# A seven-product down projection whose weight sums are made during the up projection and kept in DRAM

## The chip, the cores and the metric

The kernel runs on one core of a Trainium2 chip. The metric is device time of one execution in microseconds (us): the median of the runs shown. The core has five engines with a queue of instructions each: TensorE (PE, matrix products), VectorE (DVE), ScalarE (ACT), GpSimd (POOL) and SyncE (SP, which here only issues transfers between DRAM and the on-chip memory SBUF). An engine works its queue in order; a semaphore holds an instruction until what it needs is there. Products are accumulated in eight banks of PSUM.

## The reference

One encoder block on 512 tokens of width 1024. The part that the change touches is the gated MLP at the end, `D_FF` = 2816:

```python
def conv_ffn(h, w_up, dw_w, dw_b, w_down):
    gu = depthwise_conv(h @ w_up, dw_w, dw_b)
    gate, up = gu[..., :D_FF], gu[..., D_FF:]
    return (jax.nn.silu(gate) * up) @ w_down
...
        x = x + merged @ w_out[l]
        h2 = rms_norm(x, norm2_g[l])
        x = x + conv_ffn(h2, w_ffn_up[l], ffn_dw_w[l], ffn_dw_b[l], w_ffn_down[l])
    return rms_norm(x, norm_f_g)
```

Ahead of it lie a convolution branch and an attention branch, their merge and the product with `w_out`; neither version differs there.

## The kernel before

**Products in three.** Each float32 operand is split into a high and a low half, and a product is made as three matmuls (`mm3`, lines L219, L222, L223: high by high, high by low, low by high). A weight tile of 128x1024 is split by `halve`: ACT copies the high half (L187), DVE subtracts it from the weight to get the low half (L190). Activations are split alike by `split` (ACT L227, DVE L228).

**Weights.** A list `chunks` names all weight tiles in the order of their use. SP loads each into a ring of four buffers called `raw` (L179); `halve` fills a ring of four called `unit`. `weight(name)` prepares the tile asked for and up to two chunks after it. A raw buffer can be loaded again when its last reader is done.

**Up projection.** 44 tiles `wu0` to `wu43` of 24 matmuls 128x512 each. After a tile, ACT (L892) and DVE (L893, L895) do the convolution over tokens; after every second one DVE multiplies gate and up (L900); after every fourth, that is for each of the 11 pairs of inner tiles, POOL makes four sums of activations of 128x256 (`act_sums`, L851 to L854).

**Down projection.** For each pair the two-by-two blocks (tokens by output columns) are multiplied by a scheme with seven products in place of eight. The accumulators are `psd[p, t]`, `p` one of the products 6, 7, 1, 5 and `t` one of two token tiles. A first half (chunks `d1_i`, 24 matmuls a pair) adds to all four; a second half (`d2_i`, 18 matmuls a pair, the last three pairs in another order) goes on in 1, 7 and 5. Between the halves `u2` and `v` are formed from the accumulators (L934 to L936), and POOL adds them to the residual `x1` (L938, three a token tile); the second half's first matmul into a bank waits until its old value was read.

The scheme needs sums of weights. `prep_1` makes two 128x512 sums on DVE (L858, L860) and one on POOL (L859) after the weights' landing, stores one to DRAM (`t2d`, L861) for the second half, then halves (`w_d1b`, `w_d1a`). `prep_2` loads `t2d` and makes a further sum (L870), then halves (`w_d`, `uc`). The order of instructions on each engine is set by the framework's scheduler from the program order and its own estimates.

Of the kernel before, what the change touches and what calls it, by code (L numbers as in the profile page):

```python
# [87 lines left out]
def block_kernel(ctx, tc, xT, xtok, posb, pk, g2b, gfb, w_small, w_a, w_gate, w_q, w_kv,  # L88
# [47 lines left out]
        chunks.append((f"wm{n}", w_mo[n], D))  # L136
    for n in range(KD):
        chunks.append((f"wo{n}", w_o[n], D))
    for n in range(2 * NF):
        chunks.append((f"wu{n}", w_up[n], D))  # L140


    t2d = dram.tile([NPAIR, P, 512], F32, name="t2d")
    for n in range(NPAIR):
        chunks.append((f"d1_{n}", None, 2))
    for n in range(NPAIR):
# [5 lines left out]
    for nm, src, w in chunks:  # L152
        first_raw.append(len(raws))
        first_unit.append(nu)
        if src is not None:
            raws.append((src, w))
            nu += 1
            continue
        n = int(nm[3:])
        if nm[1] == "1":  # L160
            raws.append((w_dn[2 * n], D))
            raws.append((w_dn[2 * n + 1][:, 512:D], 512))
            nu += 2
        else:
            raws.append((w_dn[2 * n + 1], D))
            raws.append((t2d[n], 512))
            nu += 1
# [5 lines left out]
    PREP_AHEAD = 2  # L173

    def load_to(i):
        while len(loaded) <= min(i, len(raws) - 1):
            src, w = raws[len(loaded)]
            raw = wst.tile([P, 1024], F32, tag="raw", name=f"raw{len(loaded)}")
            nc.sync.dma_start(raw[:, :w], src)  # L179
# [15 lines left out]
    def prep_to(i, pin=False):  # L195
        while state["prep"] <= min(i, len(chunks) - 1):
            c = state["prep"]
            r = first_raw[c]
            load_to(r + NRAW - 1)
            nm, src, w = chunks[c]  # L200
            if src is not None:
                u = hold[nm](nm) if nm in hold else unit(nm)
                ready[nm] = halve(u, loaded[r], w, pin)
            else:
                ready[nm] = (prep_1 if nm[1] == "1" else prep_2)(int(nm[3:]), *loaded[r:r + 2])
            state["prep"] += 1
# [641 lines left out]
    def act_sums(i):  # L848

        a, b = act1[i], act2[i]  # L850
        G.tensor_tensor(out=a[:, 2], in0=a[:, 1], in1=b[:, 1], op=ADD)  # L851
        G.tensor_tensor(out=a[:, 3], in0=a[:, 2], in1=a[:, 0], op=SUB)
        G.tensor_tensor(out=a[:, 1], in0=a[:, 0], in1=a[:, 1], op=SUB)
        G.tensor_tensor(out=b[:, 2], in0=b[:, 0], in1=a[:, 3], op=SUB)  # L854

    def prep_1(i, ra, rb_):

        V.tensor_tensor(out=rb_[:, 512:], in0=rb_[:, 0:512], in1=ra[:, 512:], op=SUB)  # L858
        G.tensor_tensor(out=ra[:, 512:], in0=ra[:, 512:], in1=ra[:, 0:512], op=SUB)  # L859
        V.tensor_tensor(out=rb_[:, 0:512], in0=rb_[:, 512:], in1=ra[:, 0:512], op=ADD)  # L860
        nc.sync.dma_start(t2d[i], rb_[:, 0:512])  # L861
        ub = halve(unit(f"d1b_{i}"), rb_, 1024)
        at = asp.tile([P, 2, 4, HS], F32R, tag="as", name=f"as1_{i}")
        split((at[:, 0], at[:, 1]), act1[i])
        ua = halve(unit(f"d1a_{i}"), ra, 1024)
        return at, ua, ub

    def prep_2(i, ra, rb_):

        V.tensor_tensor(out=rb_[:, 0:512], in0=ra[:, 0:512], in1=rb_[:, 0:512], op=SUB)  # L870
        at = dp.tile([P, 2, 3, HS], F32R, tag="as", name=f"as2_{i}")
# [76 lines left out]
    for i in range(NPAIR - LATE):  # L948
        w = weight(f"d2_{i}")
        for p in (1, 7, 5):  # L950
            for t in range(2):
                second(w, t, (p,), stop=i == NPAIR - LATE - 1 and (p, t) == (7, 1))
# [137 lines left out]
```

## Time and profile before

| | us |
|---|---|
| median of 3 runs | 715.92 (715.63 to 716.55) |
| the profiled execution | 718.99 |
| its span, first to last instruction | 717.2 |
| PE busy in the span | 691.9 (96%) |
| DVE, ACT, POOL busy | 513.1, 358.5, 166.2 |
| mean granted TensorE clock | 0.989 of full speed |
| read from and written to DRAM | 74.10 MB, 4.98 MB |

PE is the engine that is nearly always busy. What another engine does shows in the time only where PE waits for it, or where the granted clock of PE falls.

### The profile page before, as it was taken

What the parts mean: (1) busy time and instruction counts of PE and PEld (TensorE: products, weight loads), DVE (VectorE), ACT (ScalarE), POOL (GpSimd) and SP (SyncE); (2) the same over time, 40 slices, a digit from 0 to 9 for tenths busy, and PEclk for the clock granted to TensorE, in tenths of its full rate; (3) what the DMA queues carried; (4) which work ended last, traced back from release to release, by engine and by line L of the source; (5) the groups of instructions that cost most, each with busy time, mean ns of one, the idle gap of its engine ahead of it and who ended that gap; (6) DMA issues with size and microseconds to landing.
All of it is one profiled execution on the core that took longest, in us unless ns stands there. A gap on an engine that the chain in (4) does not pass through costs nothing. (4 is left out here: it accounts for less than half of the span.)

```text
span 717.2 us, 8863 instructions
## 1 busy us (share of the span) xinstructions
PE 691.9 (96%) x3273; PEld 579.0 (81%) x3273; DVE 513.1 (72%) x679; ACT 358.5 (50%) x551; POOL 166.2 (23%) x208
## 2 busy tenths in 40 slices
PE   8999899999999999999999999999999998998994
PEld 8987788888888888888888888888888886786883
DVE  4767799996789986854555654555555679799985
ACT  5758656534688962433344433433333344455552
POOL 1152347702045400001101111101111125123202
PEclk9999999999999999999999999999999999899998
DMA  8803212354310162270133323323322322555533
GB/s 275 313 31 121 85 67 89 106 148 129 89 30 31 59 205 89 89 235 0 59 90 107 97 90 99 107 88 91 116 88 89 104 93 84 175 176 190 181 128 118
DMA packets 26444, 81.76 MB, mean 114 GB/s; under 512 B 3232, under 2 KB 3360, under 8 KB 26400
## 3 DMA queue, kind: packets, MB, share of 16 engines
q1 hardware_dynamic: 25536, 78.30, 33.8%
q10 hardware_dynamic: 864, 2.88, 1.2%
q8 instruction: 26, 0.43, 0.3%
q14 instruction: 18, 0.15, 0.1%
HBM read 74.10 MB, written 4.98 MB: 110 GB/s over the span
## 5 line engine op out<-in xcount | busy, mean ns | idle before, releaser
L223 PE MATMUL pu<-h,w_wu 128*128 128x512 f32 (+2 forms) x360 | 138.7, 385 | 0.0
L222 PE MATMUL pu<-h,w_wu 128*128 128x512 f32 (+2 forms) x360 | 138.7, 385 | 0.0
L219 PE MATMUL pu<-h,w_wu 128*128 128x512 f32 (+2 forms) x360 | 138.3, 386 | 0.3 <-ACT h L227 0.3
L893 DVE SCALAR_TENSOR_TENSOR u<-pu,pkt,u 128x511 f32<-128x511 f32 x44 | 33.0, 749 | 88.0 <-ACT u L892 88.0
L892 ACT ACTIVATE u<-pu,pkt 128x512 f32<-128x512 f32 x44 | 34.2, 777 | 109.9 <-PE pu L223 109.8
L219 PEld LDWEIGHTS pu<-h,w_wu 128*128 128x128 f32 x360 | 67.4, 188 | 13.9 <-ACT h L227 0.5
L223 PEld LDWEIGHTS pu<-h,w_wu 128*128 128x128 f32 x360 | 67.6, 188 | 13.5
L222 PEld LDWEIGHTS pu<-h,w_wu 128*128 128x128 f32 x360 | 67.6, 188 | 13.4
L190 DVE TENSOR_TENSOR w_wu<-raw,w_wu 128x1024 fp32r<-128x1024 f32 x44 | 54.2, 1233 | 4.7 <-ACT w_wu L187 4.7
L491 DVE SCALAR_TENSOR_TENSOR acc<-cv,pkt,acc 128x502 f32<-128x502 f32 (+10 forms) x84 | 57.1, 736 | 0.3
L489 POOL TENSOR_TENSOR cv<-prod,cv 128x510 f32<-128x510 f32 (+4 forms) x32 | 46.3, 1451 | 42.8 <-ACT prod L486 41.2
L851 POOL TENSOR_TENSOR act<-act,act 128x256 f32<-128x256 f32 x11 | 8.8, 796 | 189.7 <-DVE act L900 189.7
L219 PE MATMUL pgt<-hn,w_wg 128*128 128x512 f32 x128 | 50.2, 392 | 0.0
L223 PE MATMUL pgt<-hn,w_wg 128*128 128x512 f32 x128 | 49.9, 389 | 0.0
L222 PE MATMUL pgt<-hn,w_wg 128*128 128x512 f32 x128 | 49.8, 389 | 0.0
L187 ACT ACTIVATE w_wu<-raw 128x1024 fp32r<-128x1024 f32 x44 | 46.2, 1050 | 5.5 <-PE pso L223 2.9
L228 DVE TENSOR_TENSOR as<-act,as 128x1024 fp32r<-128x1024 f32 (+1 forms) x22 | 29.4, 1339 | 11.2 <-ACT as L227 11.2
L227 ACT ACTIVATE as<-act 128x1024 fp32r<-128x1024 f32 (+1 forms) x22 | 20.8, 948 | 30.7 <-PE psd L223 21.2
L895 DVE SCALAR_TENSOR_TENSOR u<-pu,pkt,u 128x511 f32<-128x511 f32 x44 | 33.0, 750 | 1.4
L486 ACT ACTIVATE prod<-cv,pkt 128x510 f32<-128x510 f32 (+4 forms) x32 | 22.9, 717 | 21.3 <-POOL cv L489 19.3
L677 POOL TENSOR_SCALAR pr<-pr,nm 128x512 f32<-128x512 f32 x32 | 22.1, 694 | 42.6 <-DVE nm L676 39.1
L799 POOL TENSOR_TENSOR r<-ssq 128x1 f32<-128x1 f32 x7 | 1.8, 254 | 129.3 <-ACT hp L796 129.3
(288 smaller groups left out, 1690.2 us busy)
## 6 DMA issues: line engine op xcount, KB each, us to landing
raw<-in_w_up_dram SPq DMA_DIRECT2D x44, 512.0 KB, 3.5
raw<-in_w_dn_dram SPq DMA_DIRECT2D x22, 512.0 KB, 3.5
raw<-in_w_gate_dram SPq DMA_DIRECT2D x16, 512.0 KB, 3.4
raw<-in_w_a_dram SPq DMA_DIRECT2D x8, 512.0 KB, 5.1
raw<-in_w_o_dram SPq DMA_DIRECT2D x8, 512.0 KB, 3.5
raw<-in_w_dn_dram SPq DMA_DIRECT2D x11, 256.0 KB, 3.1
t2d<-raw SPq DMA_DIRECT2D x11, 256.0 KB, 3.0
raw<-t2d SPq DMA_DIRECT2D x11, 256.0 KB, 3.5
```

What stands on the lines that cost most here:

```text
L187: x = A.activation(u[:, 0, :w], raw[:, :w], AF.Copy)
L190: x = V.tensor_tensor(out=u[:, 1, :w], in0=raw[:, :w], in1=u[:, 0, :w].bitcast(F32), op=SUB)
L219: i = T.matmul(ps, st[0], mv[0], start=start, stop=False, skip_group_check=go_on)
L222: T.matmul(ps, st[0], mv[1], start=False, stop=False, skip_group_check=go_on)
L223: T.matmul(ps, st[1], mv[0], start=False, stop=stop, skip_group_check=go_on)
L228: V.tensor_tensor(out=pair[1], in0=src, in1=pair[0].bitcast(F32), op=SUB)
L486: x = A.activation(p[:, lo:hi], u[:, lo + d:hi + d], AF.Copy, scale=w)
L489: return G.tensor_tensor(out=acc[:, lo:hi], in0=p[:, lo:hi], in1=acc[:, lo:hi], op=ADD)
L491: return V.scalar_tensor_tensor(out=acc[:, lo:hi], in0=u[:, lo + d:hi + d], scalar=w, in1=acc[:, lo:hi], op0=MULT, op1=ADD)
L892: A.activation(u, ps, AF.Identity, scale=w(1), bias=par("fb", n))
L893: V.scalar_tensor_tensor(out=u[:, 1:S], in0=ps[:, 0:S - 1], scalar=w(0), in1=u[:, 1:S], op0=MULT, op1=ADD)
L895: V.scalar_tensor_tensor(out=u[:, 0:S - 1], in0=ps[:, 1:S], scalar=w(2), in1=u[:, 0:S - 1], op0=MULT, op1=ADD)
```

## The change

A new chunk `d0_k` stands after `wu(4k+2)` in the list. It loads both down tiles of pair k (512 KB each), and DVE makes four sums of 128x512 in place (L217 to L220 of the changed kernel). SP stores both buffers to a DRAM tile `tsum` (L205). `d1_i` and `d2_i` then load finished sums, so `prep_1` and `prep_2` make none. The four activation sums of a pair (now L869 to L872) and the six adds to `x1` (now L950) go from POOL to DVE. The first half takes its products in the order 6, 5, 1, 7. The second half's first two pairs are interleaved. A limit that kept down tiles from being prepared before the last up tile falls away. The matmuls are the same in number and shape.

```diff
+    tsum = dram.tile([NPAIR, 2, P, 1024], F32, name="tsum")
     for n in range(2 * NF):
         chunks.append((f"wu{n}", w_up[n], D))
-    t2d = dram.tile([NPAIR, P, 512], F32, name="t2d")
+        if n % 4 == 2:
+            chunks.append((f"d0_{n // 4}", None, 0))
...
+        wa, wb, ta, tb = w_dn[2 * n], w_dn[2 * n + 1], tsum[n, 0], tsum[n, 1]
+        if nm[1] == "0":
+            raws += [[(wa, 0, D)], [(wb, 0, D)]]
+        elif nm[1] == "1":
+            raws += [[(ta, 0, D)], [(wa[:, 0:512], 0, 512), (tb[:, 512:D], 512, 512)]]
         else:
+            raws += [[(wb, 0, D)], [(tb[:, 0:512], 0, 512)]]
...
             load_to(r + NRAW - 1)
+            while stores:
+                nc.sync.dma_start(*stores.pop(0))
...
+    def prep_0(i, ra, rb_):
+
+        l, r = slice(0, 512), slice(512, 1024)
+        V.tensor_tensor(out=rb_[:, r], in0=rb_[:, r], in1=ra[:, r], op=SUB)
+        V.tensor_tensor(out=ra[:, r], in0=ra[:, r], in1=ra[:, l], op=SUB)
+        V.tensor_tensor(out=ra[:, l], in0=rb_[:, r], in1=ra[:, l], op=ADD)
+        V.tensor_tensor(out=rb_[:, l], in0=rb_[:, l], in1=ra[:, l], op=SUB)
+        stores.extend([(tsum[i, 0], ra), (tsum[i, 1], rb_)])
...
-        G.tensor_tensor(out=a[:, 2], in0=a[:, 1], in1=b[:, 1], op=ADD)
...
+        V.tensor_tensor(out=a[:, 2], in0=a[:, 1], in1=b[:, 1], op=ADD)
...
     def prep_1(i, ra, rb_):
 
-        V.tensor_tensor(out=rb_[:, 512:], in0=rb_[:, 0:512], in1=ra[:, 512:], op=SUB)
-        G.tensor_tensor(out=ra[:, 512:], in0=ra[:, 512:], in1=ra[:, 0:512], op=SUB)
-        V.tensor_tensor(out=rb_[:, 0:512], in0=rb_[:, 512:], in1=ra[:, 0:512], op=ADD)
-        nc.sync.dma_start(t2d[i], rb_[:, 0:512])
-        ub = halve(unit(f"d1b_{i}"), rb_, 1024)
+        ua = halve(unit(f"d1a_{i}"), ra, 1024)
         at = asp.tile([P, 2, 4, HS], F32R, tag="as", name=f"as1_{i}")
         split((at[:, 0], at[:, 1]), act1[i])
-        ua = halve(unit(f"d1a_{i}"), ra, 1024)
+        ub = halve(unit(f"d1b_{i}"), rb_, 1024)
         return at, ua, ub
 
     def prep_2(i, ra, rb_):
 
-        V.tensor_tensor(out=rb_[:, 0:512], in0=ra[:, 0:512], in1=rb_[:, 0:512], op=SUB)
+        ua = halve(unit(f"d2_{i}"), ra, 1024)
...
-            G.tensor_tensor(out=dst, in0=dst, in1=src, op=ADD)
+            V.tensor_tensor(out=dst, in0=dst, in1=src, op=ADD)
...
+    ws = [weight(f"d2_{i}") for i in range(2)]
+    for i, p in [(0, 1), (1, 1), (0, 7), (0, 5), (1, 7), (1, 5)] + [
```

On DVE, one stretch of the up projection before (two tiles; `w_wu` is the low half of a weight, `pu` the accumulator, `u` the convolution's result, `act` the gated product):

```order
L893 SCALAR_TENSOR_TENSOR u_3917<-pu_3887,pkt,u_3917 128x511
L895 SCALAR_TENSOR_TENSOR u_3917<-pu_3887,pkt,u_3917 128x511
L190 TENSOR_TENSOR w_wu_3960<-raw_3848,w_wu_3960 128x1024
L893 SCALAR_TENSOR_TENSOR u_3951<-pu_3921,pkt,u_3951 128x511
L895 SCALAR_TENSOR_TENSOR u_3951<-pu_3921,pkt,u_3951 128x511
L190 TENSOR_TENSOR w_wu_3994<-raw_3888,w_wu_3994 128x1024
L900 TENSOR_TENSOR act_4_3294<-u_3917,u_3951 128x512
```

The same two tiles after the change, with the new sums of weights (L217 to L220) and the last of the four sums of activations of the pair before (L872):

```order
L872 TENSOR_TENSOR act_3_3310<-act_3_3310,act_3_3299 128x256
L906 SCALAR_TENSOR_TENSOR u_3963<-pu_3927,pkt,u_3963 128x511
L908 SCALAR_TENSOR_TENSOR u_3963<-pu_3927,pkt,u_3963 128x511
L194 TENSOR_TENSOR w_wu_4010<-raw_3933,w_wu_4010 128x1024
L906 SCALAR_TENSOR_TENSOR u_4001<-pu_3967,pkt,u_4001 128x511
L217 TENSOR_TENSOR raw_4042<-raw_4042,raw_4008 128x512
L908 SCALAR_TENSOR_TENSOR u_4001<-pu_3967,pkt,u_4001 128x511
L194 TENSOR_TENSOR w_wu_4044<-raw_3968,w_wu_4044 128x1024
L913 TENSOR_TENSOR act_4_3300<-u_3963,u_4001 128x512
L218 TENSOR_TENSOR raw_4008<-raw_4008 128x512
L219 TENSOR_TENSOR raw_4008<-raw_4042,raw_4008 128x512
L220 TENSOR_TENSOR raw_4042<-raw_4042,raw_4008 128x512
```

Eight DVE instructions a pair are new there, and one that waits for a transfer (L217) stands in the middle of a tile's convolution.

On SP, the transfers of one pair in the up projection after the change (before, `raw<-in_w_up` alone, one after the other):

```order
L183 DMA raw_3700<-in_w_dn_dram 128x1024
L183 DMA raw_3734<-in_w_dn_dram 128x1024
L183 DMA raw_3774<-in_w_up_dram 128x1024
L205 DMA tsum<-raw_3700 128x1024
L205 DMA tsum<-raw_3734 128x1024
L183 DMA raw_3779<-in_w_up_dram 128x1024
L183 DMA raw_3814<-in_w_up_dram 128x1024
L183 DMA raw_3816<-in_w_up_dram 128x1024
```

Four transfers a pair became eight, and three of the up weights' loads stand behind the stores.

On DVE, the place between the halves before (`w_d`, `uc` are halves of second-half weights; 934 to 936 read the accumulators):

```order
L934 TENSOR_TENSOR u_0_5376<-psd_0_4939,u_0_5376 128x512
L870 TENSOR_TENSOR raw_5326<-raw_5324,raw_5326 128x512
L190 TENSOR_TENSOR w_d_1_5346<-raw_5324,w_d_1_5346 128x1024
L228 TENSOR_TENSOR uc_5349<-raw_5326,uc_5349 128x512
L935 TENSOR_TENSOR v_5377<-psd_0_4931,u_0_5376 128x512
L870 TENSOR_TENSOR raw_5340<-raw_5338,raw_5340 128x512
L936 TENSOR_TENSOR v_5377<-psd_0_4947,v_5377 128x512
L934 TENSOR_TENSOR u_1_5385<-psd_1_4943,u_1_5385 128x512
```

And after (L946 to L948 are the same three reads, L950 the adds to `x1`):

```order
L946 TENSOR_TENSOR u_0_5451<-psd_0_5044,u_0_5451 128x512
L246 TENSOR_TENSOR uc_5479<-raw_5416,uc_5479 128x512
L947 TENSOR_TENSOR v_5452<-psd_0_5052,u_0_5451 128x512
L950 TENSOR_TENSOR x_0_2907<-x_0_2907,u_0_5451 128x512
L948 TENSOR_TENSOR v_5452<-psd_0_5036,v_5452 128x512
L950 TENSOR_TENSOR x_2_2909<-x_2_2909,u_0_5451 128x512
L950 TENSOR_TENSOR x_2_2909<-x_2_2909,v_5452 128x512
L946 TENSOR_TENSOR u_1_5460<-psd_1_5048,u_1_5460 128x512
L194 TENSOR_TENSOR w_d_2_5473<-raw_5414,w_d_2_5473 128x1024
L947 TENSOR_TENSOR v_5461<-psd_1_5056,u_1_5460 128x512
L950 TENSOR_TENSOR x_1_2908<-x_1_2908,u_1_5460 128x512
L948 TENSOR_TENSOR v_5461<-psd_1_5040,v_5461 128x512
```

Between the first read of token tile 0 and its second one stood a sum, a halving of 128x1024 and a split of 128x512; now only a split of 128x512 stands there. The adds to `x1` stand ahead of the reads of token tile 1.

## Rows read from the trace of the kernel before

**Rows 1.** The page: busy time of an engine, share of the span, instructions.
```profile
PE 691.9 (96%) x3273; PEld 579.0 (81%) x3273; DVE 513.1 (72%) x679; ACT 358.5 (50%) x551; POOL 166.2 (23%) x208
```
**Rows 2.** Waits of PE: waiting <- releaser: us in total, times, longest.
```profile
PE psd L222 <- DVE w_d1b L190: 3.9, 1, 3.9
PE psd L219 <- DVE v L935: 3.3, 1, 3.3
PE psq L219 <- ACT w_ws L187: 1.4, 1, 1.4
PE ct L444 <- ACT sg L519: 1.2, 1, 1.2
```
**Rows 3.** Stretches: us, busy time of each engine, granted clock, DMA share, GB/s.
```profile
60.00:125.00 65.00, 62.24 (x284) 50.84 (x283) 60.40 (x78) 41.94 (x60) 32.37 (x26) 1.00 0.29 92
355.00:560.00 205.00, 205.00 (x911) 169.93 (x911) 112.56 (x134) 80.57 (x98) 25.90 (x36) 1.00 0.31 95
...
606.00:610.00 4.00, 0.13 (x2) 0.08 (x1) 4.00 (x4) 1.24 (x2) 2.12 (x1) 0.87 0.00 0
610.00:616.00 6.00, 6.00 (x15) 4.69 (x16) 5.96 (x7) 2.00 (x2) 0.17 (x1) 0.52 0.54 179
...
664.00:690.00 26.00, 26.00 (x116) 21.50 (x116) 25.23 (x30) 14.84 (x19) 4.53 (x3) 1.00 0.64 210
```
**Rows 4.** Timeline of PE, first half: start, us, [idle before <- releaser].
```profile
589.35 0.39 PE L219 MATMUL psd<-w_d1b,as 128*128 128x512 f32 x1
...
605.67 0.39 PE L219 MATMUL psd<-w_d1b,as 128*128 128x512 f32 x1
609.92 0.79 PE L222 MATMUL psd<-w_d1b,as 128*128 128x512 f32 x1 [3.87 <-DVE w_d1b L190]
...
615.95 0.39 PE L219 MATMUL psd<-w_d1a,as 128*128 128x512 f32 x1
```
**Rows 5.** Timeline of DVE at that place.
```profile
605.84 0.69 DVE L858 TENSOR_TENSOR raw<-raw,raw 128x512 f32<-128x512 f32 x1 [1.64 <-DMA raw<-in_w_dn_dram]
...
607.59 2.28 DVE L190 TENSOR_TENSOR w_d1b<-raw,w_d1b 128x1024 fp32r<-128x1024 f32 x1
609.79 1.21 DVE L190 TENSOR_TENSOR w_d1a<-raw,w_d1a 128x1024 fp32r<-128x1024 f32 x1
```
**Rows 6.** Timeline of POOL at that place.
```profile
606.66 2.12 POOL L859 TENSOR_TENSOR raw<-raw 128x512 f32<-128x512 f32 x1 [3.02 <-DVE raw L858]
```
**Rows 7.** Timeline of PE between the halves.
```profile
656.79 0.39 PE L223 MATMUL psd<-w_d,as 128*128 128x512 f32 x1
660.48 0.77 PE L219 MATMUL psd<-uc,as 128*128 128x512 f32 x1 [3.31 <-DVE v L935]
...
663.60 0.39 PE L223 MATMUL psd<-w_d,as 128*128 128x512 f32 x1
```
**Rows 8.** Timeline of DVE between the halves.
```profile
655.74 1.18 DVE L870 TENSOR_TENSOR raw<-raw,raw 128x512 f32<-128x512 f32 x1 [0.73 <-DMA raw<-t2d]
656.84 2.29 DVE L190 TENSOR_TENSOR w_d<-raw,w_d 128x1024 fp32r<-128x1024 f32 x1
...
659.66 0.68 DVE L935 TENSOR_TENSOR v<-psd,u 128x512 f32<-128x512 f32 x1
```
**Rows 9.** Timeline of POOL between the halves.
```profile
655.08 2.97 POOL L938 TENSOR_TENSOR x<-x,u 128x512 f32<-128x512 f32 x2 [6.38 <-DVE u L934]
```
**Rows 10.** Groups of DVE, whole span: count, busy us, mean ns, idle before.
```profile
L981 DVE TENSOR_TENSOR x<-psl,x 128x256 f32<-128x256 f32 x2 | 0.8, 416 | 0.0
```
**Rows 11.** DMA issues of the page: count, KB each, us from issue to landing.
```profile
raw<-in_w_up_dram SPq DMA_DIRECT2D x44, 512.0 KB, 3.5
...
t2d<-raw SPq DMA_DIRECT2D x11, 256.0 KB, 3.0
```
**Rows 12.** Waits of SP's queue.
```profile
SPq L179 <- DVE w_wu L190: 240.8, 44, 29.5
...
SPq L179 <- DMA t2d<-raw: 20.5, 8, 3.0
```

More of the change, by code (lines that the diff above doesn't have):

```diff
@@ L155, in block_kernel @@
         if src is not None:
-            raws.append((src, w))
+            raws.append([(src, 0, w)])
             nu += 1
@@ L159, in block_kernel @@
         n = int(nm[3:])
[L160 to L163, printed above, removed]
-        else:
-            raws.append((w_dn[2 * n + 1], D))
-            raws.append((t2d[n], 512))
-            nu += 1
+        wa, wb, ta, tb = w_dn[2 * n], w_dn[2 * n + 1], tsum[n, 0], tsum[n, 1]
[3 more added lines that the diff above has]
+            raws += [[(ta, 0, D)], [(wa[:, 0:512], 0, 512), (tb[:, 512:D], 512, 512)]]
+        else:
+            raws += [[(wb, 0, D)], [(tb[:, 0:512], 0, 512)]]
+        nu += w
     first_unit.append(nu)
@@ L173, in block_kernel @@
     PREP_AHEAD = 2
+    stores = []
     def load_to(i):
         while len(loaded) <= min(i, len(raws) - 1):
-            src, w = raws[len(loaded)]
             raw = wst.tile([P, 1024], F32, tag="raw", name=f"raw{len(loaded)}")
-            nc.sync.dma_start(raw[:, :w], src)
+            for src, c0, w in raws[len(loaded)]:
+                nc.sync.dma_start(raw[:, c0:c0 + w], src)
             loaded.append(raw)
@@ L204, in prep_to @@
             else:
-                ready[nm] = (prep_1 if nm[1] == "1" else prep_2)(int(nm[3:]), *loaded[r:r + 2])
+                ready[nm] = prep[nm[1]](int(nm[3:]), *loaded[r:r + 2])
             state["prep"] += 1
+    def prep_0(i, ra, rb_):
[5 more added lines that the diff above has]
+        stores.extend([(tsum[i, 0], ra), (tsum[i, 1], rb_)])
+    prep = {"0": prep_0}
     def weight(nm):
@@ L210, in weight @@
         i = o
-        while i < min(o + PREP_AHEAD, state["cap"], len(chunks) - 1) \
-                and first_unit[i + 2] - first_unit[o] <= NUNIT:
+        most = min(NUNIT, first_unit[o + 1] - first_unit[o] + PREP_AHEAD)
+        while i < min(state["cap"], len(chunks) - 1) \
+                and first_unit[i + 2] - first_unit[o] <= most:
             i += 1
@@ L850, in act_sums @@
         a, b = act1[i], act2[i]
-        G.tensor_tensor(out=a[:, 2], in0=a[:, 1], in1=b[:, 1], op=ADD)
-        G.tensor_tensor(out=a[:, 3], in0=a[:, 2], in1=a[:, 0], op=SUB)
-        G.tensor_tensor(out=a[:, 1], in0=a[:, 0], in1=a[:, 1], op=SUB)
-        G.tensor_tensor(out=b[:, 2], in0=b[:, 0], in1=a[:, 3], op=SUB)
+        V.tensor_tensor(out=a[:, 2], in0=a[:, 1], in1=b[:, 1], op=ADD)
+        V.tensor_tensor(out=a[:, 3], in0=a[:, 2], in1=a[:, 0], op=SUB)
+        V.tensor_tensor(out=a[:, 1], in0=a[:, 0], in1=a[:, 1], op=SUB)
+        V.tensor_tensor(out=b[:, 2], in0=b[:, 0], in1=a[:, 3], op=SUB)
     def prep_1(i, ra, rb_):
-        V.tensor_tensor(out=rb_[:, 512:], in0=rb_[:, 0:512], in1=ra[:, 512:], op=SUB)
-        G.tensor_tensor(out=ra[:, 512:], in0=ra[:, 512:], in1=ra[:, 0:512], op=SUB)
-        V.tensor_tensor(out=rb_[:, 0:512], in0=rb_[:, 512:], in1=ra[:, 0:512], op=ADD)
-        nc.sync.dma_start(t2d[i], rb_[:, 0:512])
-        ub = halve(unit(f"d1b_{i}"), rb_, 1024)
+        ua = halve(unit(f"d1a_{i}"), ra, 1024)
         at = asp.tile([P, 2, 4, HS], F32R, tag="as", name=f"as1_{i}")
         split((at[:, 0], at[:, 1]), act1[i])
-        ua = halve(unit(f"d1a_{i}"), ra, 1024)
+        ub = halve(unit(f"d1b_{i}"), rb_, 1024)
         return at, ua, ub
     def prep_2(i, ra, rb_):
-        V.tensor_tensor(out=rb_[:, 0:512], in0=ra[:, 0:512], in1=rb_[:, 0:512], op=SUB)
+        ua = halve(unit(f"d2_{i}"), ra, 1024)
         at = dp.tile([P, 2, 3, HS], F32R, tag="as", name=f"as2_{i}")
         split((at[:, 0], at[:, 1]), act2[i])
-        ua = halve(unit(f"d2_{i}"), ra, 1024)
         uc = dp.tile([P, 2, 512], F32R, tag="uc", name=f"uc_{i}")
@@ L876, in prep_2 @@
         return at, ua, (uc[:, 0], uc[:, 1])
+    prep.update({"1": prep_1, "2": prep_2})
     for j in range(NF):
@@ L886, in block_kernel @@
                 ps = bank(f"pu{n}")
-                if n == 2 * NF - 1:
-                    state["cap"] = order[f"wu{n}"]
                 up_mm(ps, *weight(f"wu{n}"), 0, S)
@@ L903, in block_kernel @@
             act_sums(j // 2)
-    state["cap"] = len(chunks)
     close_pool("h2p")
@@ L923, in block_kernel @@
         at, ua, ub = weight(f"d1_{i}")
-        ops = [(6, 3, ub, 0), (7, 1, ub, 1), (1, 0, ua, 0), (5, 2, ua, 1)]
+        ops = [(6, 3, ua, 0), (5, 2, ua, 1), (1, 0, ub, 0), (7, 1, ub, 1)]
         if i == NPAIR - 1:
-            ops = [ops[k] for k in (0, 2, 1, 3)]
+            ops = [ops[k] for k in (0, 2, 3, 1)]
         for p, slot, w, c in ops:
@@ L946, in second @@
                 dn_mm(p, t, w[0], slot, w[src], c, False, stop, True)
[L948 to L952, printed above, removed]
+    last = NPAIR - LATE - 1
+    ws = [weight(f"d2_{i}") for i in range(2)]
+    for i, p in [(0, 1), (1, 1), (0, 7), (0, 5), (1, 7), (1, 5)] + [
+            (i, p) for i in range(2, last + 1) for p in (1, 7, 5)]:
+        if i == len(ws):
+            ws.append(weight(f"d2_{i}"))
+        for t in range(2):
+            second(ws[i], t, (p,), stop=i == last and (p, t) == (7, 1))
     late = [weight(f"d2_{i}") for i in range(NPAIR - LATE, NPAIR)]
```

## Prediction, made before the changed kernel was run

> **What bounds the kernel now.** I read the page first. PE is busy for 691.9 of 717.2 us, DVE for 513.1 [rows 1], so only PE's waits can be won back. The list of waits of PE, largest first, has two in the down projection, 3.9 us for the low half of a down weight and 3.3 us for `v`; nothing else in the whole span is above 1.4 us [rows 2]. In the up projection PE is busy for all of 205 us [rows 3], so nothing can be won there, only lost.
>
> The timeline of PE at each of the two waits shows how much time it really costs, because the granted clock falls behind it. A start every 0.2267 us is the full rhythm: the first 72 matmuls of the first half go from 589.35 to 605.67 [rows 4]. The next start is at 609.92, which is 4.25 less 0.23, so 4.02 us lost. From there the 14 intervals to 615.95 take 6.03 us and would take 3.17 at full rhythm: 2.86 lost, in a stretch whose granted clock is 0.52, the lower of the two levels (1.2 GHz for 2.4) [rows 3, 4]. Together 6.9. The check over the whole first half: from 589.35 to 656.79 lie 266 intervals, 60.30 us at full rhythm, and it took 67.44, so 7.1. I use 7.1, as it counts a small hole of 0.2 that I have not listed.
>
> Between the halves starts lie at 656.79 and 660.48: 3.69 less 0.23, so 3.46 lost. From 660.48 the next 7 intervals take 3.12 in place of 1.59, 1.53 lost [rows 7]. Together 5.0. The ceiling of the gain is thus 7.1 + 5.0 = **12.1 us**; the matmuls and what lies behind the last one are the same in both versions.
>
> **Why PE waits there.** The timelines of DVE and POOL answer it. At the first place DVE waits 1.64 us for a landing, makes L858 (0.69), then the halving that PE waits for takes 2.28 us, from 607.59 on; the next halving, same shape, takes 1.21 [rows 5]. What differs is POOL: its sum L859 runs from 606.66 to 608.78, beside the slow one [rows 6]. No transfer was under way in 606 to 610 (0 GB/s), while the quick one lies in a stretch with 179 GB/s [rows 3]; so POOL slows it, not traffic. Between the halves it is the same: L870 takes 1.18 and the halving 2.29 [rows 8] beside two POOL adds from 655.08 to 658.05 [rows 9].
>
> Here a rule of the Trainium skill can be weighed, from "SBUF — State Buffer", section "Who interferes with whom": a DVE instruction with both inputs in SBUF contends with a GpSimd instruction that reads SBUF. The trace agrees, 2.28 against 1.21 us. By it, moving POOL's sums to DVE costs less DVE time than their own length, because POOL's own work no longer stretches DVE's; were traffic the cause, 1.07 us at each place would stay, and the time would be about 2 us higher.
>
> **The change part by part.**
>
> *Sums leave the first half of the down projection.* Per pair go L858 and L860 on DVE and L859 on POOL. DVE then has three instructions a pair (two halvings and a split), 3 x 1.21 = 3.6 us [rows 5] of PE's 24 x 0.2267 = 5.44. Before they were 3.6 + 2 x 0.69 = 5.0 plus what POOL stretches, one 1.07 us each pair, about 6: more than PE needs, and this is why PE catches up with DVE after three pairs. With 3.6 DVE gains on PE, and the wait of 7.1 us goes. The pace is also freed of the store: SP's loads waited 20.5 us for `t2d<-raw` to be finished [rows 12], which now was done long before. Bytes stay: 1 MB is read a pair. Worth: −7.1.
>
> *Between the halves.* L870 (1.18), the halving (2.29) and the wait for the landing (0.73) between `u2` and `v` [rows 8] leave: 4.2 us earlier, against a wait of 3.46. The first read of tile 0 is no problem then. But the adds to `x1` now stand on DVE ahead of the reads of token tile 1. From `u2` of tile 0 to `u2` of tile 1 the order has `uc`, `v`, add, `v`, add, add and `u2`: 7 instructions of 128x512 at 0.6 to 0.69 (the rows have 0.68 and 0.69 [rows 5, 8], and a next start lies some 0.08 ahead of an end [rows 5]), that is 4.2 to 4.8 us. PE has in that time the interleaved matmuls of tile 0, four groups of three, 12 x 0.2267 = 2.7 us, and ahead of it what `u2` of tile 0 is early by. That read needs products 6 and 1, which are done 12 matmuls before the end of the first half (products 7 and 5 come behind): 2.7 us less about 1.2 for ACT's copy and the read itself, so 1.5. So 2.7 + 1.5 = 4.2 us against 4.2 to 4.8: a new wait of 0 to 0.6, at the product 1 of tile 1. Then `v` of tile 1 follows behind a halving (1.21) and has PE's six matmuls of 1.4 us and two more as cover, which just fits. I take **+0.4**, and 1.5 as the upper bound of this case. A wait of this size does not bring the clock down: PE waited 1.2 us inside 60 to 125 us, and the granted clock there was 1.00 [rows 2, 3].
>
> *The up projection gets the sums.* Per pair PE runs 96 matmuls, 21.76 us. DVE is busy for 112.56 of 205 us, so 11.95 of 21.76 [rows 3]. New are four sums of 0.69 (the price of L858, same shape [rows 5]) and four of 0.42 (the nearest row of 128x256 [rows 10]): 2.76 + 1.66 = 4.4. So 16.4 of 21.76, 75%: it fits. If each ran as slowly as beside POOL (1.18 and 0.7), it would be 19.5, which fits too.
>
> Transfers: from four of 512 KB a pair to eight, so 95 GB/s [rows 3] becomes 190. In 664 to 690 us 210 GB/s ran while PE was busy for 26.00 of 26.00 [rows 3]. Then the chain through the ring: a down tile lands (3.5 [rows 11]), DVE makes four sums (2.8, some 5 with what stands between them), the store (3.0 for 256 KB, so I take 3.5 for 512 [rows 11]), and only then can two up weights be loaded into these two buffers. That is about 12 us of a pair's 21.76; SP now waits 240.8 us for the halving to free a buffer [rows 12], so it is early. If the two transfers took 8 us each in place of 3.5, the chain would be as long as PE's pair. I cost this at nothing. What hides it is PE's own work: a weight is halved some three tiles before its use, 16 us.
>
> *Instruction L217, the new wait.* It stands between the two steps of a convolution on DVE. If its landing is late, the convolution, the next halving and the gated product behind it are held; PE meets that only when banks or units run out, two or three tiles later. At nothing, too.
>
> *The limit that falls away* lets the first down tiles be prepared earlier; it lies beside PE's last up tiles.
>
> **The sum.** 718.99 − 12.1 + 0.4 = 707.3 for an execution such as the profiled one. That lies 3.1 above the median, so for a median I take 715.92 − 12.1 + 0.4 = **704.2 us**.
>
> **The rivals.** *(a) A wait of 3 us or more stays between the halves or in the first half, and the clock falls behind it.* For it: six adds of 0.69 are new on DVE, just where PE needs it, and a wait of 3.3 brought the clock to its lower level for seven matmuls, as one of 3.9 did for 14. Against it: 4.2 us of other work leave the same place. It would give 3 to 5 back: 707 to 709.5. It decides from about 2 us more on DVE there than I count.
>
> *(b) The gain isn't there.* DVE waited 1.64 us for a landing before the first wait, and 0.73 before the second [rows 5, 8]; if the loads set the pace, finished sums don't help, and the waits stay: 715 to 717. Against it: those two are smaller than what PE lost, and the loads themselves waited for the stores of `t2d` [rows 12].
>
> *(c) Slower, through the ring in the up projection.* Stores stand on SP between loads, behind DVE's sums. If a pair needs more than 21.76 us, each of 11 pairs pays the difference; 1.1 us each cancel the gain, and 2 us give 715.9 − 12.1 + 22 = 726. From transfers of more than 8 us on it decides. The Trainium skill speaks for it, "DMA: Bandwidth & Descriptors", section "Anatomy of one DMA — SWDGE (gpsimd) path": the fixed cost of a transfer is mostly the wait until the last byte is confirmed, which can be surprisingly long where the target is HBM. The row of stores to DRAM shows 3.0 us for 256 KB, no more than loads; none of 512 KB is in this trace. By the page's figures an estimate is 2.0 + 1.2 = 3.2 us for 512 KB.
>
> **How the numbers follow.** Chances: my forecast 0.72 (703.2 to 706.5, with a new wait between nothing and 1.5 us, and the spread of the runs), (a) 0.15, (b) 0.05, (c) 0.08, of which a mild form of less than 1 us a pair would still be faster or level. What a measurement can tell from no change is 0.2%, 1.4 us. So faster 0.87, same 0.05, slower 0.08. For 8 in 10 I take 0.72 and most of (a): **702.8 to 709.5**; the lower end is the ceiling of the gain, 703.8, and 1.0 for runs and clock.
>
> **What the changed profile would show.** The 3.9 us wait for the low half of `w_d1b` is gone, and from the first to the last matmul of the first half there is no start later than the full rhythm. Halvings of 128x1024 all take about 1.2 us. PE waits for `u2` of tile 1 less than 1.5 us, with no stretch at half clock. In the up projection PE is still busy for all of each pair; DVE is at about 75%, transfers at 190 GB/s. The prediction is wrong if waits for `w_wu` appear on PE in the up projection (c), or if a wait of more than 3 us stands between the halves (a).

## The result, and the profile after

The changed kernel takes **707.62 us** (median of 4 runs, 707.52 to 708.00) against 716.23 of before beside it (715.63 to 717.61): a ratio of 0.9878 with a 95% interval of 0.9861 to 0.9895, a gain of 8.6 us. Forecast were 704.2 us and a range of 702.8 to 709.5. The profiled execution after took 707.53 us with a span of 705.7; that of before took 718.99 with 717.2. Between these two profiles it is 11.5 us, close to the 11.7 of the sum. So two numbers have to be explained: where the 11.5 come from, and why a median gained 3 less.

The page after, first part (engine, busy us, share, instructions), answers to [rows 1]:

```profile
PE 686.7 (97%) x3273; PEld 575.8 (82%) x3273; DVE 525.4 (74%) x740; ACT 359.1 (51%) x551; POOL 102.8 (15%) x147
```

POOL gave up 63 us, and DVE grew by only 12, for 61 instructions more. The list of PE's waits after, from 560 to 712 us, answers to [rows 2]; it has one row:

```profile
PE psd L237 <- DVE u L946: 0.5, 1, 0.5
```

Both waits of before are gone. The stretches after (us, busy time of each engine, granted clock, DMA share, GB/s): the up projection, the first half of the down projection, the second half up to its last full-width product.

```profile
355.00:560.00 205.00, 205.00 (x908) 169.82 (x908) 148.57 (x207) 80.85 (x98) 0.00 (x0) 1.00 0.54 187
...
588.69:648.53 59.84, 59.84 (x266) 49.55 (x265) 44.11 (x45) 36.77 (x40) 0.00 (x0) 1.00 0.58 186
648.53:692.43 43.90, 43.37 (x191) 35.32 (x190) 34.15 (x43) 22.64 (x33) 1.26 (x5) 1.00 0.44 144
```

And the same two stretches in the profile of before:

```profile
589.35:656.33 66.98, 63.11 (x265) 51.39 (x264) 59.73 (x56) 34.89 (x37) 21.46 (x14) 0.95 0.48 159
656.33:704.45 48.12, 44.81 (x191) 36.38 (x190) 42.26 (x50) 24.66 (x36) 9.89 (x11) 0.96 0.45 151
```

The first half fell from 66.98 to 59.84 us, which is 264 x 0.2267, the full rhythm without a hole. The second fell from 48.12 to 43.90. The granted clock is 1.00 in both. That is 7.1 and 4.2 us; the down projection also began 0.7 sooner, and the time after the last matmul grew by 0.5: together the 11.5. In the up projection PE is still busy for all of 205 us, with DVE at 148.57 (72%; the sum said 75%) and 187 GB/s (190).

The groups of DVE after, 575 to 665 us (count, busy, mean ns, idle before):

```profile
L194 DVE TENSOR_TENSOR w_d1a<-raw,w_d1a 128x1024 fp32r<-128x1024 f32 x11 | 13.4, 1222 | 2.2 <-ACT w_d1a L191 2.2
L194 DVE TENSOR_TENSOR w_d1b<-raw,w_d1b 128x1024 fp32r<-128x1024 f32 x11 | 13.4, 1218 | 0.0
L246 DVE TENSOR_TENSOR as<-act,as 128x1024 fp32r<-128x1024 f32 x9 | 11.0, 1224 | 10.4 <-ACT as L245 10.4
L194 DVE TENSOR_TENSOR w_d<-raw,w_d 128x1024 fp32r<-128x1024 f32 x6 | 7.3, 1219 | 1.9 <-ACT w_d L191 1.9
```

Every halving takes 1.22 us, with more traffic about than before and no POOL. The place between the halves, on DVE:

```profile
646.12 0.68 DVE L946 TENSOR_TENSOR u<-psd,u 128x512 f32<-128x512 f32 x1
647.59 0.69 DVE L246 TENSOR_TENSOR uc<-raw,uc 128x512 fp32r<-128x512 f32 x1 [0.79 <-ACT uc L245]
648.20 0.68 DVE L947 TENSOR_TENSOR v<-psd,u 128x512 f32<-128x512 f32 x1
...
651.20 0.68 DVE L946 TENSOR_TENSOR u<-psd,u 128x512 f32<-128x512 f32 x1
```

and on PE:

```profile
651.94 0.50 PE L237 MATMUL psd<-w_d,as 128*128 128x512 f32 x1 [0.53 <-DVE u L946]
652.28 0.39 PE L240 MATMUL psd<-w_d,as 128*128 128x512 f32 x1
```

`v` comes 2.08 us after the start of `u2`. Before it was 5.34, from the row of `u2` here to that of `v` [rows 8]:

```profile
654.32 0.68 DVE L934 TENSOR_TENSOR u<-psd,u 128x512 f32<-128x512 f32 x1
```

The remaining wait stands at the read of token tile 1, where it was expected, with 0.5 us and the rhythm full again two matmuls later.

The issues of transfers (count, KB each, us to landing), for [rows 11]:

```profile
raw<-in_w_up_dram SPq DMA_DIRECT2D x44, 512.0 KB, 4.7
...
tsum<-raw SPq DMA_DIRECT2D x22, 512.0 KB, 3.1
```

A store of 512 KB to DRAM takes 3.1 us; the loads of up weights, among which the stores now stand, went from 3.5 to 4.7.

### The profile page after: what moved, and what is told of

It is laid out like the page before. It is cut to its first block, busy times and chain, and to the rows that moved or that the text cites. A ratio compares the mean times of both kernels' runs of the same rounds, so it can differ in the third digit from the quotient of the medians.

```text
span 705.7 us, 8940 instructions
## 1 busy us (share of the span) xinstructions
PE 686.7 (97%) x3273; PEld 575.8 (82%) x3273; DVE 525.4 (74%) x740; ACT 359.1 (51%) x551; POOL 102.8 (15%) x147
## 4 chain that ended last, share of the span: by engine, by line
PE 84%; ACT 5%; POOL 3%; DMA 3%; DVE 3%; issue 2%; SPq 0%; POOLq 0%; ACTq 0%; DVEq 0%
PE pu L237 11%; PE pu L241 11%; PE pu L240 11%; PE pgt L237 4%; PE pgt L241 4%; PE pgt L240 4%; PE psd L241 4%; PE psd L237 4%; PE psd L240 4%; PE pso L237 2%; PE pso L240 2%; PE pso L241 2%; PE po L718 2%; PE tp L707 2%; PE pco L240 1%
## 5 line engine op out<-in xcount | busy, mean ns | idle before, releaser
L246 DVE TENSOR_TENSOR as<-act,as 128x1024 fp32r<-128x1024 f32 (+1 forms) x22 | 23.8, 1089 | 15.1 <-ACT as L245 15.1
L911 ACT ACTIVATE u<-u 128x512 f32<-128x512 f32 x22 | 13.9, 633 | 31.8 <-DVE u L908 31.8
```

Of the source, the lines that this page charges most:

```text
L246: V.tensor_tensor(out=pair[1], in0=src, in1=pair[0].bitcast(F32), op=SUB)
```

## The experiments

In what follows "the first half" is the stretch from the first matmul of the down projection to the first of the second half, and "the second half" goes on from there to the first of the narrow matmuls at the end, both by starts in the timeline of PE. They leave out the start and the tail of the kernel, which differ between executions of one kernel.

**The kernel before, three more times.** No edit.

> The kernel before, unchanged, profiled once more and timed. Theory: the profiled execution of before (718.99 us) lost more behind its two waits than its other executions (715.63 to 717.61), so the ceiling of 12.1 us read from it was some 3 us too high for the median; then this profile shows the same two waits of PE in the down projection with another length of the waits or of the half-clock stretch behind them, and over the runs a higher mean granted clock goes with a shorter span. Rival: the executions lose alike, and the difference is elsewhere (start, tail, the time around the span); then the losses between 589 and 664 us are again 12.1 us within 0.5, and the span is 717.2 within 0.5.

> The kernel before once more, unchanged, for its profile. Theory: the losses at its two waits differ from execution to execution; so far the stretch from the first matmul of the down projection to the last group took 115.1 and 114.1 us, and executions with a mean clock of 0.992 or 0.993 must have lost less, 110 to 113. Expected: a stretch between 110 and 115 us, with the shorter half-clock part at the higher mean clock. Rival: the stretch is always 114 to 115, and only the start of the kernel (588.5 to 593.6 us until the down projection begins) varies.

> The same as the run before it, for a fourth profile of the kernel before: 110 to 115 us by the theory, 114 to 115 by its rival.

The first of these was also timed: 717.76 us (median of 10) against 717.27 of the same kernel beside it, a ratio of 1.0 (0.9982 to 1.0018). Measured in the profiles, with the two kernels' other profiles beside them:

| profile of | time, us | mean clock | down projection begins | first half | second half | waits of PE there |
|---|---|---|---|---|---|---|
| before | 718.99 | 0.989 | 589.35 | 66.98 | 48.12 | 3.9, 3.3 |
| before, 2nd | 717.78 | 0.988 | 589.04 | 64.62 | 49.49 | 2.7, 3.3 |
| before, 3rd | 715.18 | 0.992 | 588.87 | 63.40 | 48.28 | 2.1, 3.3 |
| before, 4th | 721.32 | 0.986 | 591.54 | 66.79 | 48.45 | 3.6, 3.3, 0.2 |
| after | 707.53 | 0.994 | 588.69 | 59.84 | 43.90 | 0.5 |
| after, 2nd | 710.01 | 0.991 | 590.76 | 59.84 | 44.23 | 0.8 |

In the third of before the first wait costs 2.3 us in place of 4.0, and the clock does not fall behind it (timeline of PE):

```profile
605.19 0.39 PE L219 MATMUL psd<-w_d1b,as 128*128 128x512 f32 x1
607.72 0.50 PE L222 MATMUL psd<-w_d1b,as 128*128 128x512 f32 x1 [2.14 <-DVE w_d1b L190]
```

What differs among the four is the landing that DVE waits for ahead of that halving. Groups of DVE (last column: idle time before and its cause), before from 598 to 612 us:

```profile
L858 DVE TENSOR_TENSOR raw<-raw,raw 128x512 f32<-128x512 f32 x2 | 1.4, 688 | 1.6 <-DMA raw<-in_w_dn_dram 1.6
```

and the third execution of before, same stretch:

```profile
L858 DVE TENSOR_TENSOR raw<-raw,raw 128x512 f32<-128x512 f32 x2 | 1.4, 680 | 0.0
```

In the order of the table DVE waited 1.6, 0.5, 0.0 and 1.3 us for that landing, and PE 3.9, 2.7, 2.1 and 3.6: 2.1 to 2.4 us that are always there, and the landing's lateness on top. Where PE's wait was 2.1 the clock stayed; where it was 2.7 or more it fell behind it. The stretches behind the wait, in the third execution and in the second (columns as above):

```profile
607.72:612.00 4.28, 4.28 (x19) 3.55 (x20) 4.28 (x5) 2.01 (x2) 0.00 (x0) 1.00 0.75 221
```

```profile
609.22:612.80 3.58, 3.58 (x10) 2.84 (x9) 3.58 (x5) 2.00 (x2) 0.00 (x0) 0.52 0.85 291
```

Between the halves the wait is 3.3 each time, with a stretch at the lower level behind it each time. Both halves together took 115.1, 114.1, 111.7 and 115.2 us: the rival of a fixed loss is refuted for the first half and holds for the length of the second wait. Over the four, the first half lost 5.6 us on the mean (65.45 less 59.84), not 7.1.

**POOL's sums on DVE, nothing else changed.**

```diff
-        G.tensor_tensor(out=a[:, 2], in0=a[:, 1], in1=b[:, 1], op=ADD)
+        V.tensor_tensor(out=a[:, 2], in0=a[:, 1], in1=b[:, 1], op=ADD)
...
-        G.tensor_tensor(out=ra[:, 512:], in0=ra[:, 512:], in1=ra[:, 0:512], op=SUB)
+        V.tensor_tensor(out=ra[:, 512:], in0=ra[:, 512:], in1=ra[:, 0:512], op=SUB)
...
-            G.tensor_tensor(out=dst, in0=dst, in1=src, op=ADD)
+            V.tensor_tensor(out=dst, in0=dst, in1=src, op=ADD)
```

> The kernel before with its POOL sums (L851 to L854, L859, L938) on DVE; the sums are still made in the down projection and t2d is still stored there. Theory that both parts of the change are needed: DVE has 2 halvings, a split and 3 sums a pair, 3 x 1.2 + 3 x 0.65 = 5.6 us against PE's 5.44, so DVE falls behind and PE still waits once in the first half, 1 to 4 us; the halvings are back at 1.2 us; a gain of 2 to 6 us on before (710 to 714). Rival, that POOL beside DVE is the whole cause: both waits go and the time is 707.6 within 1. Rival, that the landings are: both waits stay, time within 1 of before.

> The kernel before with POOL's sums on DVE, again, against the changed kernel on the same chip. Theory: 0.8 us slower than the changed kernel by its profile (104.6 against 103.7), so that the difference is between 0 and 1.6 us, at the edge of what can be measured. Rival: the sums in DRAM are worth nothing once POOL is off; no difference within 0.3 us.

Measured: 709.99 and 710.28 us, ratios 0.9885 (0.9863 to 0.9907) and 0.9895 (0.9869 to 0.9921). My theory fell: I expected a wait of 1 to 4 us in the first half, and there is none; the rival of POOL as the whole cause comes closest. It took 59.84 us in both profiles, as in the changed kernel, though DVE had all three sums of a pair to make. Stretches of the first of these profiles:

```profile
600.00:620.00 20.00, 20.00 (x89) 16.54 (x89) 19.88 (x25) 10.28 (x10) 0.00 (x0) 1.00 0.49 159
620.00:645.00 25.00, 25.00 (x112) 20.70 (x111) 24.59 (x28) 15.24 (x15) 0.00 (x0) 1.00 0.56 191
```

DVE is busy for 24.59 of 25 us and still keeps up; it has nothing to spare. The length of its list for a pair can be read from one halving of `w_d1b` to the next (timeline of DVE):

```profile
619.93 1.22 DVE L228 TENSOR_TENSOR as<-act,as 128x1024 fp32r<-128x1024 f32 x1
621.20 1.23 DVE L190 TENSOR_TENSOR w_d1b<-raw,w_d1b 128x1024 fp32r<-128x1024 f32 x1
...
626.68 1.23 DVE L190 TENSOR_TENSOR w_d1b<-raw,w_d1b 128x1024 fp32r<-128x1024 f32 x1
```

It is 5.48 us against PE's 5.44, a little under the 5.6 expected, as a start mostly lies some 0.08 ahead of the end before it. What it falls behind by, 0.04 a pair, its lead covers. The second half took 44.72 and 45.98 us, against 43.90 and 44.23 of the changed kernel. PE's waits there in the first profile:

```profile
PE psd L219 <- DVE v L935: 0.7, 1, 0.7
PE psd L219 <- ACT as L227: 0.6, 1, 0.6
```

In the second they are 1.6 us for the same `as` and 0.9 for the high half of a weight `w_d` on ACT. So taking POOL off alone removes most of the loss. On the same chip the changed kernel took 709.24 and this one 710.28; the executions lie side by side (708.22 to 710.01, and 710.01 to 711.63), but the two intervals overlap. The profiles of the second half alone put 0.5 to 2.1 us between them.

**The changed kernel with its activation sums and adds on POOL**, that is the rest of the change without what left POOL: the finished sums, but also the new order of products and the interleaved pairs.

```diff
-        V.tensor_tensor(out=a[:, 2], in0=a[:, 1], in1=b[:, 1], op=ADD)
+        G.tensor_tensor(out=a[:, 2], in0=a[:, 1], in1=b[:, 1], op=ADD)
...
-            V.tensor_tensor(out=dst, in0=dst, in1=src, op=ADD)
+            G.tensor_tensor(out=dst, in0=dst, in1=src, op=ADD)
```

> The changed kernel with the four activation sums of a pair and the six adds to x1 back on POOL; the sums of weights stay in DRAM. Theory: the finished sums carry the first half, DVE has 3.6 of 5.44 us to do there, so no wait comes back in the first half; between the halves POOL's adds stretch one or two of DVE's instructions to about twice their length but take 3 to 4 us off DVE's own list, so PE waits 0 to 1.5 us; time 707.6 within 1. Rival, that POOL beside DVE is the whole cause: a wait of 2 us or more comes back between the halves, and the time rises by 3 us or more.

Measured: 709.01 us, ratio 0.987 (0.9845 to 0.9894). First half 59.84, second half 44.78 us, with one wait of 1.0. The time lies 1.4 over the 707.6 expected, outside the 1 given; the unedited changed kernel was not timed beside it (on another chip it took 709.24, last experiment), so this miss says little. The rest is as the theory said: the finished sums carry the first half, and POOL's adds cost 0.6 to 0.9 us between the halves. A split of 128x512 takes 1.59 us beside them and 0.69 without (the row of `uc` above):

```profile
648.96 1.59 DVE L246 TENSOR_TENSOR uc<-raw,uc 128x512 fp32r<-128x512 f32 x1 [0.33 <-ACT uc L245]
```

Each half of the change alone thus gives nearly the whole gain: they are two ways to take the same load off DVE, and their gains don't add. What the new order of products and the interleaving give by themselves no run shows.

**Each of POOL's sums alone on DVE, in the kernel before** (one execution each): only the activation sums, only the sum of weights, only the adds to `x1` (each the lines of the first diff that name it).

> The kernel before with only the activation sums (L851 to L854) on DVE; L859 and the adds to x1 stay on POOL. Theory: the last pair's four sums run on POOL from 593.8 to 600 us, beside DVE's first splits and halvings of the down projection, which take 1.75 and 3.17 (two of 128x768) there in place of 1.2 and 1.8; without them DVE is some 2.5 us ahead less 1.4 for its own sums, so the first wait falls from 2.7 to 3.9 to 1 to 2.5 us; the second wait stays at 3.3. Rival, that L859 alone makes the first wait: it stays at 2.7 to 3.9.

> The kernel before with only L859 on DVE. Theory: the halving just ahead of the first wait is back at 1.2 us from 2.28, and the sum itself costs DVE 0.6; the first wait falls by 0.5 to 1.5 us from 2.7 to 3.9, but does not vanish, since the act sums have slowed what lies ahead; the second wait stays at 3.3. Rival, that L859 alone makes the first wait: it is gone or under 0.5 us.

> The kernel before with only the six adds to x1 (L938) on DVE; act_sums and L859 stay on POOL. Theory that POOL beside DVE makes both waits, each through its own instructions: the wait in the first half stays (2.5 to 4 us and its half-clock stretch), between the halves the halving that took 2.29 is back at 1.2 and the wait there falls from 3.3 to 1 us or less; 115 to 114 us from the first matmul of the down projection to the last full-width product falls by 3.5 to 5. Rival, that the landing of t2d and L870 make the second wait: it stays above 2.5 us.

Measured: 715.06, 717.00 and 719.50 us; first half 63.75, 64.10 and 65.65, second 48.13, 47.65 and 49.28 us. All three lie close to what before itself spans. The waits say more. Activation sums on DVE:

```profile
PE psd L219 <- DVE v L935: 3.3, 1, 3.3
...
PE psd L222 <- DVE w_d1b L190: 1.2, 1, 1.2
```

The first wait is under the 2.1 that before never undercut; it also stands one pair later, at 610.30 us, and DVE waited for no landing there. The second is as before. But the first half still lost 3.9 us, and the rows of POOL, ACT and DVE show why:

```profile
599.18 5.63 POOL L859 TENSOR_TENSOR raw<-raw 128x512 f32<-128x512 f32 x1 [12.85 <-DVE raw L858]
```

```profile
604.84 1.06 ACT L187 ACTIVATE w_d1a<-raw 128x1024 fp32r<-128x1024 f32 x1 [3.17 <-POOL raw L859]
```

```profile
605.93 1.23 DVE L190 TENSOR_TENSOR w_d1a<-raw,w_d1a 128x1024 fp32r<-128x1024 f32 x1 [2.27 <-ACT w_d1a L187]
...
610.64 1.21 DVE L190 TENSOR_TENSOR w_d1b<-raw,w_d1b 128x1024 fp32r<-128x1024 f32 x1
...
614.24 2.32 DVE L228 TENSOR_TENSOR as<-act,as 128x1024 fp32r<-128x1024 f32 x1
616.48 1.21 DVE L190 TENSOR_TENSOR w_d1b<-raw,w_d1b 128x1024 fp32r<-128x1024 f32 x1
```

First POOL's own sum took 5.63 us by the profile and held ACT's copy of the weight, and that held DVE for 2.27 us. Then each pair takes DVE 5.84 us (from 610.64 to 616.48, and so on to the end), since the split beside POOL's sum takes 2.32 in place of 1.22. PE needs 5.44, so it follows DVE's pace, about 0.4 later a pair, in waits too short for the list:

```profile
617.26 0.39 PE L219 MATMUL psd<-w_d1b,as 128*128 128x512 f32 x1
617.74 0.50 PE L222 MATMUL psd<-w_d1b,as 128*128 128x512 f32 x1
```

The kernel before has the same 5.84 a pair from its sixth pair on (620.53 to 626.37 us, and so on); there the lead that PE's long wait and its lower clock gave DVE mostly covers it. Giving this sum of 128x512 to POOL thus makes DVE's list 0.36 us a pair longer than keeping it on DVE: 5.84 against the 5.48 of the kernel without POOL. The sum of weights on DVE:

```profile
PE psd L219 <- DVE v L935: 2.4, 1, 2.4
PE psd L222 <- DVE w_d1b L190: 2.3, 1, 2.3
```

Here DVE waited 1.7 us for the landing, with which before had 3.9, so 1.5 were saved; neither alone makes the wait, and the theory that both share in it holds. That the second wait fell to 2.4 was not expected. The adds alone:

```profile
PE psd L222 <- DVE w_d1b L190: 3.9, 1, 3.9
PE psd L219 <- ACT as L227: 2.6, 1, 2.6
PE psd L219 <- ACT w_d L187: 1.6, 1, 1.6
```

The wait for `v` is gone, as expected, but 1.6 us come back for the next weight and 2.6 near the end, so the second half got no shorter: the expected 3.5 to 5 us did not come. At the late wait ACT splits the activations behind a split of `uc`, and that one waits for the sum L870 (timeline of ACT):

```profile
693.11 0.63 ACT L227 ACTIVATE uc<-raw 128x512 fp32r<-128x512 f32 x1 [1.29 <-DVE raw L870]
693.65 0.83 ACT L227 ACTIVATE as<-act 128x768 fp32r<-128x768 f32 x1
```

With finished sums in DRAM, L870 isn't there. The same wait for `as` is part of what is left in the kernel without POOL (0.6 and 1.6 us), and the finished sums in DRAM remove it.

**The adds to `x1` behind the reads of both token tiles.**

```diff
-        for dst, src in ((x1[t][:, 512:D], u2), (x1[t + 2][:, 0:512], u2), (x1[t + 2][:, 512:D], v)):
-            V.tensor_tensor(out=dst, in0=dst, in1=src, op=ADD)
+        adds += [(x1[t][:, 512:D], u2), (x1[t + 2][:, 0:512], u2), (x1[t + 2][:, 512:D], v)]
+    for dst, src in adds:
+        V.tensor_tensor(out=dst, in0=dst, in1=src, op=ADD)
```

> The changed kernel with the six adds to x1 written behind the reads of both token tiles (and so set later on DVE). Theory: the 0.5 us wait of PE for u2 of tile 1 comes from the three adds that stand ahead of it; it goes, and the time falls by 0.5 to 0.9 us. Rival: PE waits for v or for the halving of the third pair's weight in its place; no difference beyond 0.3 us.

Measured: 709.52 us, ratio 0.9878 (0.985 to 0.9906); second half 43.94, wait 0.6. No gain. The read of `u2` of tile 1 now starts 1.59 us after the second half's first matmul in place of 2.67; but the scheduler also moved the matmul that waits for it forward, to 2.33 us from 3.41. So the run doesn't tell whether the adds are the cause of the remaining wait; it stays open, for 0.5 us.

**Each store of sums four times.** It tests the rival of a ring that becomes the bound.

```diff
-        stores.extend([(tsum[i, 0], ra), (tsum[i, 1], rb_)])
+        stores.extend([(tsum[i, 0], ra), (tsum[i, 1], rb_)] * 4)
```

> The changed kernel with each store of a pair's sums issued four times in a row to the same place. Tests the rival of the prediction that the ring of raw buffers in the up projection can become the bound. With one store the chain (landing 3.5, sums 5, store 3.1) takes about 12 us of a pair's 21.76; three more pairs of stores, each waiting for the last one, add 9 to 13 us. Theory: 21 to 25 us, at the edge: PE waits for w_wu between nothing and 4 us a pair, and the time is 707.6 to 745. If the stores overlap (queue, not receipt, sets the pace), 4 MB more a pair at 313 GB/s, the fastest slice of the page of before, are 12 to 13 us: the same edge. Rival, the ring has much more slack than worked out: no wait for w_wu at all, time within 1.5 of 707.6.

Measured: 719.51 us in one execution, some 10 us over the changed kernel's runs. Stretches (as above):

```profile
355.00:560.00 205.00, 204.89 (x907) 169.37 (x907) 139.57 (x196) 76.39 (x93) 0.00 (x0) 1.00 0.83 290
560.00:590.00 30.00, 26.77 (x115) 20.91 (x114) 21.91 (x31) 10.42 (x13) 0.00 (x0) 1.00 0.88 312
```

and its waits of PE, 560 us on:

```profile
PE psd L237 <- DVE u L908: 3.6, 1, 3.6
PE pu L237 <- ACT w_wu L191: 2.2, 2, 1.3
PE pu L241 <- DVE w_wu L194: 1.1, 2, 0.5
```

With 3 MB more a pair, at 290 GB/s, PE loses 0.1 of 205 us. But the sums fall behind meanwhile. The first of them (L217), first and last start, in the changed kernel and here:

```profile
L217 DVE TENSOR_TENSOR raw<-raw,raw x11: 685/691/693, 317.4 to 558.0; 128x512 f32<-128x512 f32 x11
```

```profile
L217 DVE TENSOR_TENSOR raw<-raw,raw x11: 683/693/693, 317.6 to 581.4; 128x512 f32<-128x512 f32 x11
```

The last pair's comes 23.4 us later. From the second pair on these starts lie 24.0 us apart on the mean (364.99 to 581.38 over nine pairs), where PE takes 21.76 a pair; in the changed kernel they lie 21.5 apart (364.92 to 557.98). PE lives on its lead until the last pairs, where it waits for `w_wu`, and then once at the start of the down projection. So the rival's mechanism is real, and with 24 us its edge lies within the 21 to 25 that I had worked out. The change itself, at 21.5, keeps PE's pace.

**The changed kernel once more.** No edit.

> The changed kernel, unchanged, on the same chip as the runs beside it. Theory: its down projection takes 103.7 us within 0.5 in this profile too, since no wait there is long enough to bring the clock down; its times spread only by what the start of the kernel adds. Against before a gain of 8.5 to 11 us (the ratio 0.985 to 0.988). Rival: the gain in the timed runs stays at 8.7 or less because the changed kernel loses time in executions that were not profiled; then its clock is under 0.992 in some of them and they are 2 us longer.

Measured: 709.24 us (708.22 to 710.01) against 718.15 (716.70 to 720.78), ratio 0.9872 (0.9843 to 0.9901), 8.9 us. First half 59.84, second 44.23, one wait of 0.8. The clock was 0.991 and 0.992, one of the two signs named for the rival, but the profiled one of these executions (0.991) lost only 0.3 us more in the down projection. The rest of what it has more than the first profile of after lies ahead of it, 2.1 us until the down projection begins; the granted clock over the first 100 us was 0.98, against 1.00 there.

## Why the prediction was right, and where its size was off

*What bounds the kernel.* Right. The two waits and the stretches behind them were nearly all that PE lost in the down projection; with them gone it runs the first half without a hole.

*Why PE waits.* Right that POOL beside DVE stretches DVE's instructions: halvings take 1.22 us where POOL rests, at 186 GB/s too. This agrees with the rule of the Trainium skill, "SBUF — State Buffer", section "Who interferes with whom". Right, too, that with POOL beside it DVE's list for a pair is more than PE needs: it was worked out as about 6 us and is 5.84, against 5.44. But at 0.4 a pair this makes, as an estimate, only some 1.2 us of the wait in three pairs. The rest the prediction did not name as such: the start of the down projection, where POOL's last activation sums ran beside DVE's splits and put DVE behind, and the landing of a weight. That landing I had put aside as a rival, and it made up 0 to 1.6 of the wait's 2.1 to 3.9 us.

*Sums leave the first half: −7.1.* The wait went entirely, but the size is that of one execution. Over four profiles of before the loss was 7.1, 4.8, 3.6 and 7.0 us, mean 5.6.

*Between the halves: −5.0 + 0.4.* Measured: 48.59 on the mean of four before, 44.07 on the mean of two after, −4.5. The new wait stood at the read of tile 1 and was 0.5 and 0.8 us, without a fall of the clock.

*The up projection at nothing.* Right: PE lost nothing there. DVE's share (72% for 75%) and the traffic (187 GB/s for 190) came out nearly as costed; the store took 3.1 us for an assumed 3.5, the loads 4.7.

*From the profiled execution to the median.* This is the step that failed: "That lies 3.1 above the median, so for a median I take 715.92 − 12.1 + 0.4". It took the 3.1 us for an offset that both kernels have, and so took a loss of 12.1 off a median execution that had not lost as much. The forecast for an execution such as the profiled one, 707.3, met the profiled one of after, 707.53; but its median is 707.62, the same. The executions of before differ by 6.1 us (715.18 to 721.32), and a part of that is the very wait that the change removes: the profiled one had the longest of four, and the one of 715.18 us lost 3.6 in the first half where it had lost 7.1. With the means over four profiles the sum would have been −5.6 − 4.5 = −10.1. The tail after the last matmul's start grew by 0.5 us in both profiles of after (11.24 against 10.72), for which no run gives the reason; that leaves 9.6, and the means of the profiled executions lie 9.55 apart (718.32 and 708.77), the down projection beginning at 589.7 in both. The step from 9.6 to the timed 8.6 and 8.9 us stays open: the time until the down projection begins alone varies by 3.9 us over the profiles (588.54 to 592.47, without the kernel of four stores), and few executions were profiled. So the median lies outside the 703.2 to 706.5 of the forecast itself, in the band of rival (a), which did not come: that it lies within the stated range is partly luck.

*The rivals.* (a) did not come: the waits left are under 1 us. (b) holds in part, as said. (c) lies where it was put, and the change is clear of it; a store of 512 KB took 3.1 us where the estimate was 3.2. The section of the Trainium skill that was cited for it, "DMA: Bandwidth & Descriptors", "Anatomy of one DMA — SWDGE (gpsimd) path", is on transfers that GpSimd issues; here SP issued them.

## What to carry to other kernels

Sum up what a wait costs with the stretch at the lower clock behind it, but over several profiled executions: a wait that depends on a landing differs by microseconds from one to the next, and the size of its removal is its mean, not the one profile's. Where an engine is late because another slows it and because its list is long, either remedy may do the whole work; try each alone before paying for both, here 23 MB more of traffic for 0.5 to 2.1 us. And before giving an engine's work to a second one, measure what it does to the first: here DVE's list got longer by what POOL took over. And look for what the removed wait had covered: the adds moved alone gave their gain back at two other places.

## What the runs showed of the hardware that was not expected

PE waited 2.1 us without a fall of its granted clock in one execution, and 2.3 (only the sum of weights on DVE) and 2.7 us with one, 0.8 us after it went on (0.2267 us a start at the full level, 0.4267 at the lower). DVE at 98% busy for 25 us held back nothing. A sum of 128x512 on POOL lengthened a split of 128x1024 on DVE from 1.22 to 2.32 us, more than the 0.69 that the sum takes on DVE itself. The transfer queues carried 290 GB/s over 205 us, stores to DRAM among them, while PE lost 0.1 us.
